# Attention's 64-partition products widened with zeros, and the compressed branch taken two heads at a time, in a hybrid decoder layer on one core

## The chip, the cores and the metric

The kernel runs on one core of one Trainium2 chip. TensorE (PE) multiplies matrices, with a queue of its own for weight loads; VectorE (DVE), ScalarE (ACT) and GpSimd (POOL) do elementwise work and reductions; SyncE (SP) issues most DMAs. The metric is device time in microseconds from one launch of the whole program, lower is better. Before, three runs took 3534.8, 3547.48 and 3551.98 us; the median is 3547.48 us.

## The reference

One decoder layer over 1024 tokens of width 1024, batch 1, in float32: a mixer of three branches, then a PEER feed-forward with 16384 experts. The change touches the first two branches of the mixer.

```python
h = rms_norm(x)
proj = h @ w_in
# A: stick-breaking attention, 8 heads of 64, strictly causal
z = einsum("bhtd,bhsd->bhts", q, k) * 64 ** -0.5
after = cumsum(log_1m, reverse) - log_1m         # log_1m = log_sigmoid(-z)
a = exp(log_sigmoid(z) + after);  o = a @ v
# B: sparse attention, 8 query heads of 64, 2 groups of keys and values
s_c = q @ kc * scale - slope * dist_c            # 63 compressed keys per group
p_c = softmax(where(valid_c, s_c, NEG));  o_c = p_c @ vc
imp = einsum("bgptc,cn->bgtn", p_c, overlap)     # 16 blocks of 64 keys, the best 4 taken
o_s = softmax(q @ k[selected] - slope * dist) @ v[selected]
o_w = softmax(q @ k[window of 256] - slope * dist) @ v[window]
o = g0 * o_c + g1 * o_s + g2 * o_w
# C: HGRN2 gated recurrence;  m = sum of gated branches @ W;  x = x + m @ w_out
x = x + peer(rms_norm(x));  out = rms_norm(x)
```

## The kernel before

Tokens are cut into four parts of 256, and a part into two tiles of 128. The program has a **mixer**, in which all three branches, their projections, the output projection and the routing of the feed-forward are interleaved, and a **dense part** behind it, which multiplies 512 tokens (parts 1 and 2) with all experts. The other 512 tokens gather their experts' rows from memory one by one (L1145 and L1155 issue the gathers on POOL, L1147 and L1157 use the rows on VectorE), spread over the mixer and the dense part.

Projections (`proj`, L258) multiply 128 x 128 weight blocks with 256 tokens as three float16 products each. Attention is in float32. In a float32 product TensorE gets one instruction of the program, which the profile shows as two pairs of weight load and product; a transpose is one pair.

Order comes from three places. `sb_items`, `nsa_items` and `hg_items` give lists of items of up to four stages (logits, weights, turned, values). At step t the planner's loop runs stage 0 of item t, stage 1 of item t-1, stage 3 of item t-3 and stage 2 of item t-2, in that order. Between steps it fills in projections and routing as *pieces*, by a running account of how much TensorE and VectorE have been given. The gathers' uses on VectorE are tied to steps. Last, the framework's scheduler decides the order on each engine, and it derives the waits between engines from what each instruction reads and writes.

What the change touches:

- **Stick-breaking heads.** A pair of heads p is projected at once: `pq` (L375) copies the 128 x 256 result to `q`, head 0 on partitions 0 to 63 and head 1 on 64 to 127. `k` has the same form. `logits` (L410) multiplies the 64 partitions of one head with up to 512 keys into `z`; where the chunk holds the diagonal a bfloat16 mask product (L412) adds to it.
- **Sparse heads, queries and keys.** For a group of four heads `qh` has 81 partitions: 0 to 63 hold the query (L550), 64 to 80 hold 17 rows that give each token a penalty per block and are multiplied only with `ksel`, whose rows 64 to 80 name the block. `kwin` and `kcT` (window and compressed keys) have 64 partitions, so L659 and L571 read `qh[0:64]`; L663 reads `qh[0:81]`.
- **A tile's items** (`res` in `nsa_items`): item 0 does the compressed branch, with `c_logits` (L571), `c_norm`, `c_turn` (L617, one transpose per head, 64 compressed keys to the partitions, copied by ACT in L619) and `c_values` (L624, one product of 64 x 64 per head); item 1 selects blocks; item 2 is the first window head; item 3 holds `c_rows` alone, as stage 2: it transposes the selection (L611) and adds it to a `base` of the part into rows 64 to 80 of `qh` (L612, VectorE). Window heads (L659) 1 to 3 and the four selected heads (L663) are items 4 to 10.
- **`turn_values`** copies the compressed values of both groups to `vc` (L527) and loads `base` for the part (L528).

In the names, `ns3g1t0` is part 3, group 1, tile 0; `b2h1` is the window branch and head 1, `b1` the selected branch; `tre` and `eT` are a head's transposed weights, `ob` its output, `trp` and `pT` the transposed compressed weights, `ovc` the compressed output, `trs` the transposed selection.

## Time and profile before

| what | us |
|---|---|
| runs, lowest, median and highest | 3534.8, 3547.48, 3551.98 |
| the profiled execution | 3542.42 |
| its span, first to last instruction | 3540.6 |
| PE busy (20660 instructions) | 3248.8, 92% |
| PE weight loads busy | 2179.3, 62% |
| DVE busy (6662) | 3001.0, 85% |
| ACT busy (3162) | 1549.5, 44% |
| POOL busy (1166) | 1357.0, 38% |
| chain of waits that ended last: PE, DVE, issue, DMA | 52%, 23%, 8%, 8% |

Busy times are of the profiled execution. Products overlap in TensorE's pipeline, and a row's duration runs from the start of the product to its modelled end; what a product holds back is read from the start of the next. A row of the timeline has start, duration, engine, line, operation, the names of output and inputs, the shape (for a product rows * columns of the weights, then the moving operand) and, after x, how many alike follow one another. The chain of waits goes back from the last instruction, at each step to what released it; its shares by line say which work stood on that path. "Issue" in it is time in which the engine waited for nothing that the profile shows.

### The profile page before, as it was taken

The page shows a single profiled execution, that of the slowest core. Times are in us where ns is not written, and L with a number is a line of the kernel's source. Part 1 is how long each engine was busy: PE and PEld are TensorE (multiplying, and loading weights), DVE is VectorE, ACT ScalarE, POOL GpSimd, SP SyncE. Part 2 cuts the span into 40 slices and gives each one's busy share as a digit, 9 for nine tenths or more (in the row PEclk, how much of TensorE's full clock was granted, in tenths as well). Part 3 has the DMA queues.
Part 4 walks back from the last instruction along what each step waited for, and adds up shares of the span by engine and source line. Part 5 has one row for each costly group of instructions (what it writes and reads, how often), then busy time and mean ns, then how long its engine had stood idle before and what let it go on. Part 6 is the DMA issues. An engine that isn't in the chain of part 4 may idle for free.

```text
span 3540.6 us, 57087 instructions
## 1 busy us (share of the span) xinstructions
PE 3248.8 (92%) x20660; PEld 2179.3 (62%) x20660; DVE 3001.0 (85%) x6662; ACT 1549.5 (44%) x3162; POOL 1357.0 (38%) x1166
## 2 busy tenths in 40 slices
PE   7999999999997799999879889879999999999997
PEld 6887777777876687887666654434444444444443
DVE  6665679888789888889998878999987998898898
ACT  5776455654443454644355333233333333233332
POOL 0000001343333233223332234347764765776663
PEclk9999999999997799999677899989999999999998
DMA  8964856889977587887665899779998999999997
GB/s 305 335 239 145 304 185 226 325 306 325 354 268 240 175 299 264 313 327 275 213 204 202 301 361 333 241 265 387 387 369 315 371 381 353 378 348 361 347 369 258
DMA packets 359336, 1058.07 MB, mean 299 GB/s; under 512 B 35238, under 2 KB 107626, under 8 KB 354444
## 3 DMA queue, kind: packets, MB, share of 16 engines
q0 software_dynamic: 147456, 536.94, 42.3%
q1 hardware_dynamic: 206988, 483.93, 38.6%
q10 hardware_dynamic: 4608, 33.56, 2.4%
q8 instruction: 162, 2.65, 0.3%
q14 instruction: 122, 1.00, 0.1%
HBM read 944.19 MB, written 110.10 MB: 298 GB/s over the span
## 4 chain that ended last, share of the span: by engine, by line
PE 52%; DVE 23%; issue 8%; DMA 8%; ACT 6%; POOL 2%; SPq 0%; DVEq 0%; ACTq 0%; POOLq 0%
PE g L258 13%; PE acc L1436 10%; PE pj_mg L258 4%; DVE gacc L1157 4%; PE g L1436 3%; DVE u L1147 3%; DMA v<-in_peer_v_dram,gidx 3%; PE pj_r_hg L258 2%; DMA u<-in_peer_u_dram,gidx 2%; PE pb L258 2%; PE pj_wo L258 2%; DMA gt<-d_G 1%; POOL u L1145 1%; PE z_sb L410 1%; DVE sv L980 1%
## 5 line engine op out<-in xcount | busy, mean ns | idle before, releaser
L1155 POOL DMA_INDIRECT v<-in_peer_v_dram,gidx x421 | 551.9, 1311 | 685.6 <-DVE gacc L1157 400.8
L1145 POOL DMA_INDIRECT u<-in_peer_u_dram,gidx x417 | 520.7, 1249 | 646.2 <-DVE u L1147 415.8
L258 PE MATMUL g<-h,us 128*128 128x512 f16 x3072 | 693.0, 383 | 22.8 <-DVE ts L982 7.9
L1157 DVE SCALAR_TENSOR_TENSOR gacc<-v,act,gacc 128x1024 f32<-128x1024 f32 x421 | 537.9, 1278 | 37.4 <-DMA v<-in_peer_v_dram,gidx 32.9
L1436 PE MATMUL acc<-vs,ac 128*128 128x512 f16 x2304 | 536.9, 381 | 20.4 <-ACT vs L213 8.4
L1436 PEld LDWEIGHTS <-ac 128*128 128x128 f16 x3072 | 302.0, 98 | 410.8 <-issue 50.3
L258 PEld LDWEIGHTS <-us 128*128 128x128 f16 x3072 | 302.5, 99 | 392.4 <-issue 22.2
L1147 DVE SCALAR_TENSOR_TENSOR u<-u,gh 128x1024 f32<-128x1024 f32 x417 | 501.8, 1217 | 27.3 <-DMA u<-in_peer_u_dram,gidx 26.0
L1395 ACT ACTIVATE ge<-g 128x512 f32<-128x512 f32 x128 | 76.1, 595 | 528.6 <-PE g L258 461.6
L258 PE MATMUL pj_mg<-hT,w_mg 128*128 128x256 f16 x2304 | 274.0, 274 | 4.8 <-ACT mg L881 3.7
L258 PEld LDWEIGHTS <-w_mg 128*128 128x128 f16 x2304 | 227.1, 100 | 35.9 <-issue 9.9
L1436 PE MATMUL g<-vs,ac 128*128 128x512 f16 x768 | 184.4, 383 | 22.7 <-ACT ge L1395 21.8
L214 DVE SCALAR_TENSOR_TENSOR vs<-vraw,vs 128x1024 f16<-128x1024 f32 x128 | 154.9, 1216 | 25.6 <-ACT vs L213 25.4
L213 ACT ACTIVATE vs<-vraw 128x1024 f16<-128x1024 f32 x128 | 132.6, 1046 | 88.6 <-DMA vraw<-in_peer_v_dram 88.5
L1145 POOL DMA_INDIRECT rr_u<-in_peer_u_dram,gidx x95 | 137.3, 1445 | 84.2 <-DVE rr_u L1147 61.0
L213 ACT ACTIVATE ac<-ge 128x512 f16<-128x512 f32 x128 | 80.1, 628 | 201.6 <-DVE ge L1429 155.6
L1155 POOL DMA_INDIRECT rr_v<-in_peer_v_dram,gidx x90 | 131.3, 1459 | 93.9 <-DVE gacc L1157 69.6
L214 DVE SCALAR_TENSOR_TENSOR us<-uraw,us 128x1024 f16<-128x1024 f32 x128 | 155.5, 1216 | 6.3 <-ACT us L213 5.0
L258 PE MATMUL pb<-o,w_b 128*128 128x256 f16 x1152 | 144.5, 282 | 16.2 <-DVE sg L919 10.5
L1219 PE MATMUL gb<-hot 128*128 128x128 f16 x512 | 126.0, 294 | 32.2 <-DVE hot L1216 26.2
L1429 DVE TENSOR_TENSOR ge<-ge,gt 128x256 f32<-128x256 f32 x256 | 98.0, 419 | 57.2 <-ACT ge L1395 27.2
L258 PE MATMUL pj_r_hg<-hT,w_r_hg 128*128 128x256 f16 x1152 | 140.2, 279 | 5.2 <-ACT iv_hg L739 3.3
(1141 smaller groups left out, 6361.5 us busy)
## 6 DMA issues: line engine op xcount, KB each, us to landing
uraw<-in_peer_uT_dram SPq DMA_DIRECT2D x128, 512.0 KB
vraw<-in_peer_v_dram SPq DMA_DIRECT2D x128, 512.0 KB
w_mg<-dw SPq DMA_DIRECT2D x72, 512.0 KB
gt<-d_G SPq DMA_DIRECT2D x32, 1024.0 KB
d_G<-stages ACTq DMA_DIRECT2D x20, 1024.0 KB
w_r_hg<-dw SPq DMA_DIRECT2D x36, 512.0 KB
w_b<-dw SPq DMA_DIRECT2D x72, 256.0 KB
wr_mg<-in_wblk_dram SPq DMA_DIRECT2D x24, 512.0 KB
```

The source lines that it names most:

```text
L213: S.activation(hi, src, AF.Copy, scale=scale)
L214: V.scalar_tensor_tensor(lo, in0=src, scalar=scale, in1=hi, op0=ALU.mult, op1=ALU.subtract)
L258: P.matmul(ps, l[:, k, :], r[:, k, :], start=(i == 0), stop=(i == n - 1))
L410: P.matmul(x["z"], st["q"][b:b + 64, tl * 128:(tl + 1) * 128], st["k"][b:b + 64, r0 + c0:r0 + c1], start=True, stop=(c0 > 0))
L1145: G.indirect_dma_start(out=ur, out_offset=None, in_=a["peer_u"], in_offset=bass.IndirectOffsetOnAxis(ap=idx[:, c:c + 1], axis=0))
L1147: V.scalar_tensor_tensor(ur, in0=ur, scalar=1.0, in1=h2, op0=ALU.mult, op1=ALU.mult, accum_out=hpre[:, c:c + 1])
L1155: G.indirect_dma_start(out=vr, out_offset=None, in_=a["peer_v"], in_offset=bass.IndirectOffsetOnAxis(ap=idx[:, c:c + 1], axis=0))
L1157: V.scalar_tensor_tensor(acc, in0=vr, scalar=act[:, c:c + 1], in1=acc, op0=ALU.mult, op1=ALU.add)
L1219: P.matmul(ps[:, n, :], hs[:, 0, :, n], hs[:, 2, :, n], start=True, stop=False)
L1395: S.activation(ge, ps, AF.Gelu, scale=1.0 / (SW * SH2))
L1429: V.tensor_tensor(gv, gv, gt[:, :, i % 8, :], op=ALU.mult)
L1436: P.matmul(ps, ac[:, x, t * 128:(t + 1) * 128], v[:, y, dh * 512:(dh + 1) * 512], start=start and n == 0, stop=stop and n == 2)
```

## The change

Four tiles are made once and cleared: `kwin` and `kcT` grow to 81 partitions with zeros in the new ones; `qh` is one tile for the whole program; `qz` holds the queries of a pair of stick-breaking heads in two planes, head 0 in partitions 0 to 63 of plane 0 and head 1 in 64 to 127 of plane 1, zeros elsewhere; `vc` holds the compressed values twice, on partitions 0 to 63 for the first of two heads and on 64 to 127 for the second, with zeros in the other blocks. Then

- L410 multiplies 128 partitions (`qz` with both heads' keys), and `pq` makes two copies of 64 partitions instead of one of 128;
- L571 and L659 multiply all 81 partitions of `qh`;
- `c_turn` transposes two heads (128 columns) at once, twice, and `c_values` multiplies two heads with the two blocks of `vc`, twice;
- `base` is loaded once, for positions within a tile, with a column of the tile's offset; `c_rows` adds three terms instead of two, and moves from stage 2 to stage 3 of its item, since the window logits of its tile now read the rows that it writes.

```diff
+        load(base, a["c_base"])
...
-    kwin = per.tile([64, 2, 512], F32, name="kwin")
+    kwin = per.tile([81, 2, 512], F32, name="kwin")
+    qh = per.tile([81, 4, PARTS[0].n], F32, name="qh")
+    qz = per.tile([128, 2, PARTS[0].n], F32, name="qz")
+    vc = per.tile([128, 2, 128], F32, name="vc")
+    base = per.tile([17, 136], F32, name="base")
+    for t in (kwin[64:81], qh[64:81], qz, vc):
+        G.memset(t, 0.0)
...
-    kcT = per.tile([64, 2, 64], F32, name="kcT")
+    kcT = per.tile([81, 2, 64], F32, name="kcT")
...
-            st["q"] = W2(f"q_{nm}", (128, pt.n), tag="sbq", bufs=1)
-            S.activation(st["q"], ps, AF.Copy, scale=0.125 * PS)
+            for hh in range(2):
+                S.activation(qz[hh * 64:hh * 64 + 64, hh], ps[hh * 64:hh * 64 + 64], AF.Copy, scale=0.125 * PS)
...
-                P.matmul(x["z"], st["q"][b:b + 64, tl * 128:(tl + 1) * 128], st["k"][b:b + 64, r0 + c0:r0 + c1], start=True, stop=(c0 > 0))
+                P.matmul(x["z"], qz[:, hh, tl * 128:(tl + 1) * 128], st["k"][:, r0 + c0:r0 + c1], start=True, stop=(c0 > 0))
...
-            V.tensor_copy(st["vc"], pv)
-            st["base"] = load(per.tile([17, n], F32, tag="base", name=f"base_{nm}"), a["c_base"][:, t0:t0 + n])
+            V.tensor_copy(vc[0:64, :, 0:64], pv)
+            V.tensor_copy(vc[64:128, :, 64:128], pv)
...
-                P.matmul(zc[:, i, :], st["qh"][0:64, i, ts], kcT[:, g, :], start=True, stop=True)
+                P.matmul(zc[:, i, :], qh[:, i, ts], kcT[:, g, :], start=True, stop=True)
...
-            V.tensor_tensor(st["qh"][64:81, :, ts], kv["base"][:, ts].unsqueeze(1).to_broadcast([17, 4, 128]), tr[0:17, :].unsqueeze(1).to_broadcast([17, 4, 128]), op=ALU.add)
+            V.scalar_tensor_tensor(qh[64:81, :, ts], in0=base[:, 0:128].unsqueeze(1).to_broadcast([17, 4, 128]), scalar=base[:, 128 + ti:129 + ti], in1=tr[0:17, :].unsqueeze(1).to_broadcast([17, 4, 128]), op0=ALU.add, op1=ALU.add)
...
-            for i in range(4):
-                P.transpose(trp[:, i, :], x["s"][:, i, :], ident)
+            for i in range(2):
+                P.transpose(trp[:, i, :], x["s1"][:, 1 + i * 128:129 + i * 128], ident)
...
-            for i in range(4):
-                P.matmul(ovc[:, i, :], x["pT"][:, i, :], kv["vc"][:, g, :], start=True, stop=True)
+            for i in range(2):
+                P.matmul(ovc[:, 2 * i:2 * i + 2, :], x["pT"][:, i, :], vc[:, g, :].rearrange("p (h d) -> p h d", h=2), start=True, stop=True)
...
-        res = [[c_logits, c_norm, c_turn, c_values], [None, c_select, None, None], None, [None, None, c_rows, None]]
+        res = [[c_logits, c_norm, c_turn, c_values], [None, c_select, None, None], None, [None, None, None, c_rows]]
...
-                                P.matmul(zv[:, a:b], st["qh"][0:64, i, ts], kwin[:, g, k0:k0 + b - a], start=True, stop=True)
+                                P.matmul(zv[:, a:b], qh[:, i, ts], kwin[:, g, k0:k0 + b - a], start=True, stop=True)
```

The scheduler's order on TensorE, at tile 0 of group 1 in part 3, from the transposed compressed weights to the first selected logits. Before (the shape is the output's):

```order
L617 MATMUL trp_ns3g1t0_20107<-packed_106,s_ns3g1t0_19957 64x128 x4
L659 MATMUL z_ns3g1t0b2h2_0_20209<-kwin_152,qh_ns3g1_19470 128x384
L624 MATMUL ovc_ns3g1t0_20143<-vc_ns3_15966,pT_ns3g1t0_20112 128x64 x4
L683 MATMUL tre_ns3g1t0b2h0_0_20191<-packed_106,e_ns3g1t0b2h0_0_20089 128x128 x3
L611 MATMUL trs_ns3g1t0_20218<-packed_106,sel_ns3g1t0_20098 32x128
L659 MATMUL z_ns3g1t0b2h3_0_20222<-kwin_152,qh_ns3g1_19470 128x384
```

and now:

```order
L621 MATMUL trp_ns3g1t0_20109<-packed_106,s_ns3g1t0_19950 128x128 x2
L663 MATMUL z_ns3g1t0b2h2_0_20142<-kwin_152,qh_153 128x384
L663 MATMUL z_ns3g1t0b2h3_0_20152<-kwin_152,qh_153 128x384
L687 MATMUL tre_ns3g1t0b2h0_0_20124<-packed_106,e_ns3g1t0b2h0_0_20091 128x128 x3
L628 MATMUL ovc_ns3g1t0_20115<-vc_155,pT_ns3g1t0_20112 128x128 x2
L615 MATMUL trs_ns3g1t0_20157<-packed_106,sel_ns3g1t0_20100 32x128
```

Four transposes and four products have become two of each, and the logits of the last window head stand ahead of the transposed selection instead of behind it. (Line numbers of the changed kernel are four higher here.)

On VectorE, at the first tile of the program, around the write of the selection rows (`og` is the gated output of the compressed branch, `w_r2` and `o2` are splits of a weight and of another branch's output, `e` and `nmx` the reduction of a window head). Before:

```order
L626 TENSOR_TENSOR og_ns0g0_897<-ovc_ns0g0t0_1071,gts_ns0_442 128x256
L214 SCALAR_TENSOR_TENSOR w_r2_hg1_0_1219<-wr_r2_hg1_0_1220,w_r2_hg1_0_1219 128x1024
L214 SCALAR_TENSOR_TENSOR o2_0_1022<-sq_hg0_0_967,o2_0_1022 128x256
L612 TENSOR_TENSOR qh_ns0g0_817<-base_ns0_815,trs_ns0g0t0_1173 17x4x128
L668 ISA e_ns0g0t0b2h3_0_1212,nmx_ns0g0t0b2h3_1209<-z_ns0g0t0b2h3_0_1210,dwin_140 128x128
```

and now:

```order
L630 TENSOR_TENSOR og_ns0g0_903<-ovc_ns0g0t0_1075,gts_ns0_450 128x256
L221 SCALAR_TENSOR_TENSOR w_r2_hg1_0_1208<-wr_r2_hg1_0_1209,w_r2_hg1_0_1208 128x1024
L221 SCALAR_TENSOR_TENSOR o2_0_1028<-sq_hg0_0_973,o2_0_1028 128x256
L672 ISA e_ns0g0t0b2h3_0_1244,nmx_ns0g0t0b2h3_1241<-z_ns0g0t0b2h3_0_1242,dwin_140 128x128
L616 SCALAR_TENSOR_TENSOR qh_153<-base_156,trs_ns0g0t0_1247 17x4x128
```

The row write has moved behind the reduction of the last window head. Over the whole program VectorE's gather rows stand at the same places as before: between the row writes of any two tiles their count so far differs by at most four, and 417 of 1024 stand ahead of the first of the dense part's rows in both.

More of the change, by code (lines that the diff above doesn't have):

```diff
@@ L519, in compress @@
                 P.matmul(pk[:, :, 0:ncb], st["cw", which][:, j, :], st["xp", which][:, j, :, 0:ncb], start=(j == 0), stop=(j == 15))
-            V.tensor_copy(dst[:, :, c0:c1], pk[:, :, 0:ncb])
+            V.tensor_copy(dst[0:64, :, c0:c1], pk[:, :, 0:ncb])
         def turn_values():
-            st["vc"] = SM(f"vc_{nm}", [64, 2, 64], bufs=1)
             pv = ps_mm.tile([64, 2, 64], F32, tag="mm", name=f"pvc_{nm}")
@@ L544, in pq @@
         def pq(i):
-            if i == 0:
-                st["qh"] = W2(f"qh_{gn}", (81, 4, pt.n), tag="qh", bufs=1)
             ps = proj(B_NQ + 2 * g + i, hTs[pt.i], f"nq{i}_{gn}", pt)
             for u in range(2):
-                S.activation(st["qh"][0:64, 2 * i + u, :], ps[u * 64:u * 64 + 64, :], AF.Copy, scale=0.125 * PS / SLOPES[4 * g + 2 * i + u])
+                S.activation(qh[0:64, 2 * i + u, :], ps[u * 64:u * 64 + 64, :], AF.Copy, scale=0.125 * PS / SLOPES[4 * g + 2 * i + u])
         return [lambda: pq(0), lambda: pq(1)]
@@ L611, in c_rows @@
             P.transpose(tr[0:32, :], x["sel"], ident)
-            V.tensor_tensor(st["qh"][64:81, :, ts], kv["base"][:, ts].unsqueeze(1).to_broadcast([17, 4, 128]), tr[0:17, :].unsqueeze(1).to_broadcast([17, 4, 128]), op=ALU.add)
+            V.scalar_tensor_tensor(qh[64:81, :, ts], in0=base[:, 0:128].unsqueeze(1).to_broadcast([17, 4, 128]), scalar=base[:, 128 + ti:129 + ti], in1=tr[0:17, :].unsqueeze(1).to_broadcast([17, 4, 128]), op0=ALU.add, op1=ALU.add)
         def c_turn():
-            trp = ps_tr.tile([64, 4, 128], F32, tag="tr", name=f"trp_{tn}")
-            for i in range(4):
-                P.transpose(trp[:, i, :], x["s"][:, i, :], ident)
-            x["pT"] = W2(f"pT_{tn}", (64, 4, 128))
+            trp = ps_tr.tile([128, 2, 128], F32, tag="tr", name=f"trp_{tn}")
+            for i in range(2):
+                P.transpose(trp[:, i, :], x["s1"][:, 1 + i * 128:129 + i * 128], ident)
+            x["pT"] = W2(f"pT_{tn}", (128, 2, 128))
             S.activation(x["pT"], trp, AF.Copy)
@@ L662, in logits @@
                         last = c1 == W
-                        P.matmul(zv, st["qh"][0:81, i, ts], ksel[0:81, g, c0:c1], start=True, stop=not last)
+                        P.matmul(zv, qh[:, i, ts], ksel[0:81, g, c0:c1], start=True, stop=not last)
                         if last:
@@ L1489, in _constants @@
     tt = np.arange(T)
-    b = np.zeros((17, T), f)
-    b[0:16] = 64 * np.arange(16)[:, None] - tt[None, :]
-    b[16] = 1
+    b = np.zeros((17, 136), f)
+    b[0:16, 0:128] = 64 * np.arange(16)[:, None] - np.arange(128)[None]
+    b[0:16, 128:136] = -128 * np.arange(8)[None]
+    b[16, 0:128] = 1
     c["c_base"] = b
```

## The prediction

> **What bounds the kernel now.** I read first the span and the busy time by stretch, then the chain of waits in the stretches where the changed lines run, and last the timeline of TensorE around single changed products. The profiled execution took 3542.42 us, its span is
>
> ```profile
> span 3540.6 us, 57087 instructions
> ```
>
> and the busy times by stretch are (each engine's busy us and instructions: PE, its weight loads, DVE, ACT, POOL; then granted clock, DMA share, GB/s):
>
> ```profile
> 0.00:500.00 500.00, 451.48 (x3786) 385.27 (x3787) 303.23 (x747) 316.35 (x733) 5.81 (x68) 0.97 0.73 256
> 500.00:1200.00 700.00, 633.49 (x4814) 522.12 (x4813) 620.64 (x1984) 332.70 (x833) 223.68 (x242) 0.92 0.79 275
> 1200.00:1600.00 400.00, 384.28 (x3031) 322.09 (x3031) 332.21 (x676) 211.10 (x503) 125.16 (x120) 0.97 0.83 295
> 2400.00:3541.00 1141.00, 1103.52 (x5077) 498.09 (x5074) 1037.44 (x1397) 374.59 (x505) 721.01 (x505) 0.99 0.96 355
> ```
>
> All lines that change run in the mixer, before 2000 us; the dense part behind it keeps its instructions. In the mixer two engines compete. Up to 500 us TensorE is busy 90% and VectorE 61%: TensorE leads. From 500 to 1200 us both stand near 90%, and who is late changes from piece to piece. From 1200 to 1600 us TensorE leads again with 96% against 83%. So an instruction taken off TensorE is worth its time in the first and third stretch, and little where VectorE's top-k and gather rows are late. The chain of waits, its shares by line in the whole mixer, then in the first and in the third stretch, says how much:
>
> ```profile
> by line: issue 9.5%; PE pj_mg L258 7.1%; PE pj_r_hg L258 4.1%; DVE u L1147 3.8%; DMA u<-in_peer_u_dram,gidx 3.5%; PE pb L258 3.1%; PE pj_wo L258 2.6%; DVE gacc L1157 2.5%; POOL u L1145 1.9%; PE z_sb L410 1.8%; PE pj_q_sb L258 1.4%; PE gb L1
> by line: PE pj_mg L258 13.0%; PE pj_r_hg L258 9.3%; PE pj_wo L258 4.2%; PE pb L258 3.8%; issue 3.1%; PE pj_i_hg L258 2.7%; PE pj_q_sb L258 2.7%; PE z_sb L410 2.2%; PE pj_k_sb L258 2.1%; PE pj_nq_ns0g L258 2.1%; PE pj_v_sb L258 2.1%; ACT L89
> by line: PE pj_mg L258 11.7%; PE pb L258 7.3%; PE gb L1219 5.5%; PE gb L1220 5.3%; PE pj_r_hg L258 3.3%; DVE gacc L1157 3.1%; PE z_sb L410 3.0%; PE ov_sb L440 2.7%; PE pj_wo L258 2.6%; DMA v<-in_peer_v_dram,gidx 2.6%; PE pj_q_sb L258 2.4%;
> ```
>
> The largest changed line, L410 (the logits of the stick-breaking heads), is busy in the stretches as follows (TensorE, weight loads, clock, DMA):
>
> ```profile
> 0.00:500.00 500.00, 13.59 (x40) 5.89 (x40) 0.97 0.73 256
> 500.00:1200.00 700.00, 33.01 (x64) 10.55 (x64) 0.92 0.79 275
> 1200.00:1600.00 400.00, 21.69 (x44) 6.68 (x44) 0.97 0.83 295
> 1600.00:2000.00 400.00, 28.86 (x44) 7.70 (x44) 0.78 0.67 226
> ```
>
> Of its 97.1 us, 1.8% of 2000 us = 36 us lie on the chain. In the first stretch it is 2.2% of 500 = 11 of 13.6 us (0.81), in the third 3.0% of 400 = 12 of 21.7 us (0.55), and in the other two together 13 of 61.9 us (0.21).
>
> **What a product on 64 partitions costs.** Two places of the timeline, TensorE alone (start, duration, line, shapes; "64*128" is rows times columns of weights; a float32 product takes two instructions). Durations overlap in the pipeline, so I use differences of starts:
>
> ```profile
> 1438.05 0.94 PE L683 MATMUL tre_ns3g0t0b1h<-packed,e_ns3g0t0b1h 128*128 128x128 f32 x7
> 1438.92 1.12 PE L410 MATMUL z_sb<-k_sb,q_sb 64*128 64x512 f32 x2
> 1439.97 0.23 PE L412 MATMUL z_sb<-sbmask,identb 128*128 128x128 bf16 x1
> ...
> 1592.51 0.62 PE L683 MATMUL tre_ns3g0t1b1h<-packed,e_ns3g0t1b1h 128*128 128x128 f32 x4
> 1592.97 1.02 PE L663 MATMUL z_ns3g0t1b1h<-ksel,qh_ns3g 81*128 81x512 f32 x2
> 1593.83 0.22 PE L665 MATMUL z_ns3g0t1b1h<-cmask,identb 128*128 128x128 bf16 x1
> ```
>
> Both pairs stream the same 512 columns. On 64 rows it takes 1439.97 - 1438.92 = 1.05 us, on 81 rows, which already use the whole array, 0.86 us. Weights of 64 rows are loaded only when the array stands still; those of 81 rows come in under the product before. The work ahead pays too: a transpose of 128 columns takes 0.108 us (four in 0.43 us, L617 below), so seven should take 0.76 and take 0.87 (0.11 more), four should take 0.43 and take 0.46 (0.03 more). A run of 64-row products therefore costs (1.05 + 0.11) - (0.86 + 0.03) = **0.27 us** more than the same columns on the whole array.
>
> The compressed branch, one tile:
>
> ```profile
> 1405.31 0.60 PE L617 MATMUL trp_ns3g0t<-packed,s_ns3g0t 128*64 128x128 f32 x4
> 1405.74 1.47 PE L258 MATMUL pb<-o,w_b 128*128 128x256 f16 x12
> 1407.14 0.91 PE L659 MATMUL z_ns3g0t0b2h<-kwin,qh_ns3g 64*128 64x384 f32 x2
> ...
> 1410.73 1.47 PE L258 MATMUL pb<-o,w_b 128*128 128x256 f16 x12
> 1412.14 1.10 PE L624 MATMUL ovc_ns3g0t<-vc_ns,pT_ns3g0t 64*128 64x64 f32 x8
> 1413.17 0.87 PE L683 MATMUL tre_ns3g0t0b2h<-packed,e_ns3g0t0b2h 128*128 128x128 f32 x6
> 1413.88 1.47 PE L258 MATMUL pb<-o,w_b 128*128 128x256 f16 x12
> 1415.19 1.67 PE L663 MATMUL z_ns3g0t0b1h<-ksel,qh_ns3g 81*128 81x512 f32 x4
> ...
> 1531.78 0.60 PE L258 MATMUL pj_v_sb<-hT,w_v_sb 128*128 128x256 f16 x4
> 1532.31 1.10 PE L571 MATMUL zc_ns3g0t<-kcT,qh_ns3g 64*128 64x64 f32 x8
> 1533.34 0.49 PE L849 MATMUL ov_hg<-att_hg,iv_hg 128*128 128x128 f32 x2
> ```
>
> Twelve projections ahead of an 81-row product take 1.31 us, ahead of a 64-row one 1.40 and 1.41: the same stop of 0.1 us.
>
> **The change, part by part.**
>
> 1. Stick-breaking logits (L410): 192 instructions are 96 products, nearly all alone between other work: 96 x 0.27 = 25.9 us of TensorE.
>
> 2. Window logits (L659): between these two rows, the first and the last, I count 54 unbroken runs with whole-array work on both sides: 54 x 0.27 = 14.6 us.
>
> ```profile
> 85.78 0.48 PE L659 MATMUL z_ns0g0t0b2h<-kwin,qh_ns0g 64*128 64x128 f32 x2
> 1888.04 1.65 PE L659 MATMUL z_ns3g1t1b2h<-kwin,qh_ns3g 64*128 64x384 f32 x2 [0.44 <-DVE nmx_ns3g1t1b2h L668]
> ```
>
> 3. Compressed logits (L571), 16 tiles: eight instructions take 1.03 us where eight loads of 128 columns need 0.86, and the four projections ahead take 0.53 instead of 0.44: 0.26 x 16 = 4.2 us.
>
> 4. Compressed values (L624), 16 tiles: the stop of 0.10 and 1.03 us go; two products of 128 columns, four instructions of 0.108 us, come: 0.70 x 16 = 11.2 us.
>
> 5. Transposed weights (L617): two transposes instead of four, 2 x 0.108 x 16 = 3.5 us.
>
> The sum is **59 us** of TensorE, all in the mixer. That the added rows are zeros or hold finite numbers against zero keys changes no duration: the product streams columns, as the 81-row pair shows.
>
> Added work. The query copy of L375 becomes two copies of 64 partitions, at the price (min/median/max ns) of the nearest row, L550, which copies the same shape:
>
> ```profile
> L550 ACT ACTIVATE qh_ns0g<-pj_nq_ns0g x8: 378/379/382, 75.2 to 204.6; 64x256 f32<-64x256 f32 x8
> ```
>
> There are 16 of these copies, so that is 16 x 0.38 = 6 us more on ACT, which is busy 63% of the first stretch and about half of the next two; the copy is made ahead of its logits by the planner. I cost it at nothing, with 6 us as the other end. The copy of the transposed weights halves in width, and three small loads of `base` fall away, so neither takes it up again. Four more small copies and four clears at the start are too few to count.
>
> The wait. Compressed and window logits now read rows 64 to 80 of the queries too, so the write of the selection rows (L612) has to follow the window logits of its tile; it is moved one stage back for that. In before it often starts while the last of these runs:
>
> ```profile
> 1567.89 0.91 PE L659 MATMUL z_ns3g0t1b2h<-kwin,qh_ns3g 64*128 64x384 f32 x2
> 1568.61 0.68 DVE L612 TENSOR_TENSOR qh_ns3g<-base_ns,trs_ns3g0t 17x512 f32<-17x512 f32 x1
> 1570.98 1.04 PE L663 MATMUL z_ns3g0t1b1h<-ksel,qh_ns3g 81*128 81x512 f32 x2
> ```
>
> The logits end at 1568.80, so the row write would start 0.2 us later and end at 1569.49, still 1.5 us ahead of the selected logits (L663) that wait for it. Behind it on VectorE stands a gather row, and behind that the window logits' own reduction. Bounds: nothing, if every tile has this cover; 16 x 0.91 = 15 us of VectorE, if each waited for a whole product. The row above is nearest to nothing; I take 1 us. The operation also changes from a sum of two to a sum of three at the same 17 x 512; no row shows that shape, and I take it as equal, with a doubling (16 x 0.68 = 11 us of VectorE, in the stretches where VectorE leads perhaps half of it) as the other end. On VectorE the gathers keep their places among the row writes to within four, so pacing does not shift.
>
> **How much of the 59 us arrives.** L410 is busy longer late in the mixer, where its rows are long; but what it saves goes by the run, not by the length. By runs (20 in the first stretch, 22 in the third, 54 in the others) its share on the chain is (20 x 0.81 + 22 x 0.55 + 54 x 0.21) / 96 = **0.41**. I take this for the other lines too, which come once or a few times a tile: 0.41 x 59 = 24 us, less 1 for the wait: **23 us**. From the profiled execution that gives 3519; the three runs shown have a median 5 us above it, 3547.5, so the forecast for a median is **3524**. If 15 to 40 us arrive, it lies between 3507 and 3532.
>
> **The rivals.**
>
> *VectorE takes the slack.* From 500 to 1200 us it is busy 621 of 700 us and TensorE 633; TensorE's lead there is hardly 13 us, about what L410 alone loses in that stretch (32 x 0.27 = 9 us). If the same happens in the first stretch through ACT and DMA, only the third keeps its part, 0.55 of 13 us (22 x 0.27 = 6 of L410, and a fifth of the other lines' 33), and with VectorE's possible 6 us for row writes nothing is left: 0 to 10 us, 3537 to 3553. Against it: in the first stretch VectorE is 39% idle. Chance 0.22.
>
> *Nearly all of it arrives.* If what I call off the chain only waits in turn with it, 45 to 59 us go: 3488 to 3503. For it: TensorE is above 90% nearly everywhere. Chance 0.10.
>
> *The change does only part of what it says:* the second weight load of a product still waits for the first product. Then a third of each 0.27 us stays, 150 runs x 0.09 = 13.5 us, and 0.41 of 45 us less 1 arrives, 17 us: 3530. The row of 81 rows speaks against it, since 0.86 us leaves no room for a load between its two halves. Chance 0.03. The Trainium skill states a rule of this kind (TensorE: Matmul & The Clock Gate, Part 3, "The mechanism"): weight loads overlap products in flight only when they go to another row group. By that rule whole-array loads would never overlap, and padding would not help inside a pair; the twelve projections in 1.31 us say otherwise for whole-array weights.
>
> *Slower, by the clock.* In these two rows (columns as above) VectorE leads, and in the second TensorE has fallen to a granted clock of 0.59:
>
> ```profile
> 1000.00:1100.00 100.00, 93.65 (x763) 78.03 (x761) 96.48 (x396) 42.83 (x108) 30.75 (x27) 1.00 0.79 275
> 1100.00:1200.00 100.00, 70.61 (x311) 53.16 (x311) 93.80 (x291) 42.00 (x106) 27.39 (x32) 0.59 0.50 157
> ```
>
> Less work on TensorE means more gaps there. If the first of them fell to 0.59 as well, its 93.7 us of TensorE would need 159, up to 65 us more; less the 23 that is 42 us slower: 3589. It decides from about two thirds of such a stretch on (23 + 18 of 65 us). Against it: what is taken off in 100 us of that kind is about 3 us, and where VectorE leads the clock is not paid in full. Chance 0.08.
>
> **How the numbers follow.** The forecast has 0.57, then 0.10, 0.22, 0.03 and 0.08 for the rivals in the order nearly all, VectorE, part, slower. A measurement of this kernel tells 0.5% (18 us) from no change. Faster by more than that is most of the forecast (0.50), nearly all (0.10) and some of "part": 0.62. Within it are the rest of the forecast, VectorE's case and the rest: 0.30. Slower: 0.08. The range leaves out the slower case and half of "nearly all": 3495 to 3553.
>
> **What would show it.** In the profile of the changed kernel a pair of 512 columns in L410's place should take 0.86 us from start to start, not 1.05, and the projections ahead of it should lose their 0.1 us. TensorE's work up to 2000 us should shrink by about 59 us at equal clock, and the dense part should begin some 23 us earlier and last as long. Wrong would be: selected logits that wait for the row write longer than the 1 us taken; a granted clock well below 0.97 before 500 us; or a mixer that is as long as before with more idle time on TensorE.

## The result, and the profile after

The changed kernel takes **3520.55 us** in the median of 8 runs (3510.71 to 3532.81), the kernel before 3549.73 in the median of 8 runs beside them: a ratio of **0.9924, 95% interval 0.99 to 0.9949**, that is 27 us or 0.76% less. The profiled execution of the changed kernel took 3510.71 us, the lowest of its runs, so what follows from it alone is off by some microseconds. (In one run below, "stops put in elsewhere", one of six executions took 15322 us, and its ratio goes by the other five, 3504 to 3531 us.)

Its span and the busy times by stretch (columns as before: PE, weight loads, DVE, ACT, POOL, then granted clock, DMA share, GB/s):

```profile
span 3508.9 us, 56926 instructions
...
0.00:500.00 500.00, 445.14 (x3778) 388.44 (x3779) 306.70 (x768) 319.56 (x740) 8.51 (x72) 0.96 0.73 258
500.00:1200.00 700.00, 617.71 (x4836) 523.92 (x4835) 623.10 (x1975) 343.93 (x856) 226.06 (x243) 0.92 0.80 278
1200.00:1600.00 400.00, 381.23 (x3134) 330.73 (x3133) 346.19 (x708) 223.59 (x529) 137.73 (x131) 0.99 0.88 308
1600.00:2000.00 400.00, 321.72 (x2110) 257.93 (x2109) 358.10 (x1035) 170.84 (x376) 120.61 (x103) 0.81 0.66 229
```

TensorE's busy time fell in every stretch (451 to 445, 633 to 618, 384 to 381 us), while the instructions of all engines moved ahead: between 1200 and 1600 us TensorE now does 3134 instead of 3031. Busy time per window can't show more than that, because a faster program has other work in the same window. So I compare when the same work starts in the two profiles. The projection that started at 473 us starts 3.4 us earlier, the one at 1089 us 10 us, the one at 1375 us 27 us, the one at 1694 us 29 us, and the first product of the dense part (2062 us) 26 us. Most of the gain over the kernel before thus comes between 500 and 1375 us, and little before 500 us.

The chain of waits by line, of the mixer and of its first 500 us:

```profile
by line: issue 8.5%; PE pj_mg L265 7.2%; DVE u L1151 4.5%; PE pj_r_hg L265 3.7%; DMA u<-in_peer_u_dram,gidx 3.5%; DVE gacc L1161 2.7%; PE pb L265 2.1%; POOL u L1149 2.1%; PE pj_wo L265 2.0%; DMA v<-in_peer_v_dram,gidx 1.9%; PE gb L1223 1.7%
by line: PE pj_mg L265 12.1%; PE pj_r_hg L265 7.2%; PE pj_wo L265 4.2%; PE pj_q_sb L265 3.0%; issue 3.0%; PE pj_xc_ns L265 2.6%; DMA ksel<-in_c_kblk_dram 2.5%; ACT L902 2.3%; DMA dw<-w_ng_ns 2.1%; PE pj_nq_ns0g L265 2.1%; DMA sg<-d_g 2.0%; 
```

`z_sb` (L410, now L417) is gone from the first lines of both, where it had 1.8% and 2.2%; DVE's gather rows L1151 rose from 3.8 to 4.5% of the mixer, and three DMAs stand in the first stretch's list.

The same products as before on TensorE (start, duration, line, shapes), each read from the start of the next:

```profile
1384.60 0.81 PE L663 MATMUL z_ns3g0t0b2h<-kwin,qh 81*128 81x384 f32 x2
1385.25 0.38 PE L621 MATMUL trp_ns3g0t<-packed,s_ns3g0t 128*128 128x128 f32 x2
1385.47 0.49 PE L687 MATMUL tre_ns3g0t0b2h<-packed,e_ns3g0t0b2h 128*128 128x128 f32 x3
1385.80 2.78 PE L265 MATMUL pb<-o,w_b 128*128 128x256 f16 x24
1388.42 0.81 PE L663 MATMUL z_ns3g0t0b2h<-kwin,qh 81*128 81x384 f32 x2
1389.07 0.61 PE L628 MATMUL ovc_ns3g0t<-vc,pT_ns3g0t 128*128 128x128 f32 x4
1389.51 1.47 PE L265 MATMUL pb<-o,w_b 128*128 128x256 f16 x12
...
1417.14 0.50 PE L687 MATMUL tre_ns3g0t0b1h<-packed,e_ns3g0t0b1h 128*128 128x128 f32 x3
1417.47 1.02 PE L417 MATMUL z_sb<-k_sb,qz 128*128 128x512 f32 x2
1418.33 0.22 PE L419 MATMUL z_sb<-sbmask,identb 128*128 128x128 bf16 x1
```

The 512-column pair takes 1418.33 - 1417.47 = 0.86 us and the transposes ahead of it 0.33 for three, 0.11 each: the stop of 0.27 us is gone. 24 projections ahead of window logits take 2.62 us, 0.109 each, with no stop either. Two transposes take 0.22 us, the compressed values 0.44 instead of 1.03 us and a stop. The edits do on TensorE what the prediction said.

Where, then, is the rest? The longest waits of TensorE in the mixer, first of the changed kernel, then of the kernel before (line waiting, what it waits for: us in total, times, longest):

```profile
PE z_sb L417 <- DVE r_sb L432: 32.2, 14, 13.4
PE tra_sb L438 <- ACT r_sb L433: 19.3, 14, 3.7
...
PE pb L265 <- DVE sg L923: 14.4, 11, 2.2
```

```profile
PE z_sb L410 <- DVE r_sb L425: 31.2, 12, 11.7
...
PE tra_sb L431 <- ACT r_sb L426: 9.7, 8, 2.9
...
PE pb L258 <- DVE sg L919: 8.1, 6, 2.8
```

TensorE waits twice as long for ACT's part of the stick-breaking heads, and nearly twice as long for VectorE's gates `sg`. To see the whole of it I divided TensorE's time up to the last output projection of the mixer (about 2100 us), from the start of each product to the start of the next: the time that its columns need at full clock; gaps in which the engine waited; what it took longer while the granted clock was half; and the rest, mostly stops. (Worked out from all rows of TensorE, each kernel's from one execution. The wait until the first product is left out; it is 7 us longer in the changed kernel and in the two below.)

| us | columns | stops, rest | half clock | waits |
|---|---|---|---|---|
| before | 1647.5 | 119.1 | 150.9 | 196.0 |
| changed | 1636.7 | 85.2 | 127.5 | 230.4 |
| infra (below): changed, but all products as before | 1647.5 | 119.3 | 143.1 | 210.3 |
| no padding (below) | 1636.7 | 119.5 | 141.6 | 205.0 |

45 us of columns and stops went, 23 us of half clock too, and 34 us came back as waits, 7 more at the start: 27 us in all. Of the 34, 24 are waits for ACT (80 before, 105 now), 6 for VectorE (113, 119) and 5 for DMAs.

### The profile page after: what moved, and what is told of

Same layout as the page of the kernel before. It is cut to its first block, busy times and chain, and to the rows that moved or that the text cites. A ratio compares the mean times of both kernels' runs of the same rounds, so it can differ in the third digit from the quotient of the medians.

```text
span 3508.9 us, 56926 instructions
## 1 busy us (share of the span) xinstructions
PE 3176.1 (91%) x20564; PEld 2166.0 (62%) x20564; DVE 2999.3 (85%) x6666; ACT 1554.1 (44%) x3179; POOL 1357.4 (39%) x1170
## 4 chain that ended last, share of the span: by engine, by line
PE 47%; DVE 28%; DMA 10%; issue 7%; ACT 6%; POOL 2%; SPq 0%; ACTq 0%; DVEq 0%; POOLq 0%
PE g L265 13%; PE acc L1440 9%; DVE u L1151 4%; PE pj_mg L265 4%; DVE gacc L1161 3%; PE g L1440 3%; DMA v<-in_peer_v_dram,gidx 2%; PE pj_r_hg L265 2%; DMA u<-in_peer_u_dram,gidx 2%; PE pj_wo L265 1%; DMA vraw<-in_peer_v_dram 1%; DMA gt<-d_G 1%; PE pb L265 1%; POOL u L1149 1%; DVE rr_u L1151 1%
## 5 line engine op out<-in xcount | busy, mean ns | idle before, releaser
L1151 DVE SCALAR_TENSOR_TENSOR u<-u,gh 128x1024 f32<-128x1024 f32 x417 | 504.0, 1223 | 42.0 <-DMA u<-in_peer_u_dram,gidx 41.6
L265 PEld LDWEIGHTS <-w_b 128*128 128x128 f16 x1152 | 116.5, 102 | 42.9 <-issue 21.1
```

The lines of the kernel that those rows point to most:

```text
L265: P.matmul(ps, l[:, k, :], r[:, k, :], start=(i == 0), stop=(i == n - 1))
L1151: V.scalar_tensor_tensor(ur, in0=ur, scalar=1.0, in1=h2, op0=ALU.mult, op1=ALU.mult, accum_out=hpre[:, c:c + 1])
```

## The experiments

Ratios are to the kernel before, with the 95% interval; 0.001 is 3.5 us.

An edit of the products changes one thing more: the scheduler derives its waits from what is read and written, and orders the engines anew. I compared the order of instructions in the traces, up to 2200 us. Between the changed kernel and "no padding" some 1150 of 14870 instructions stand elsewhere on TensorE, and 470 of 4760 operations on VectorE; between the two runs with the write in the third stage it is 1420 and 670. "Parts 1 to 3 alone" (120 and 30), "stops, with the wait" (130 and 60) and "65 rows" (40 and 40) have nearly the order of the changed kernel. Where the order moves, a difference of some microseconds can come from that as well, and no run here holds it fixed.

**No padding.** The changed kernel with the logits of L417, L575 and L663 on 64 partitions; everything else stays.

```diff
-P.matmul(x["z"], qz[:, hh, ...], st["k"][:, ...], ...)
+P.matmul(x["z"], qz[b:b + 64, hh, ...], st["k"][b:b + 64, ...], ...)
-P.matmul(zc[:, i, :], qh[:, i, ts], kcT[:, g, :], ...)
+P.matmul(zc[:, i, :], qh[0:64, i, ts], kcT[0:64, g, :], ...)
-P.matmul(zv[:, a:b], qh[:, i, ts], kwin[:, g, k0:k0 + b - a], ...)
+P.matmul(zv[:, a:b], qh[0:64, i, ts], kwin[0:64, g, k0:k0 + b - a], ...)
```

> The changed kernel with its padding undone in the products alone: stick-breaking, compressed and window logits multiply 64 partitions again (of the same tiles), and everything else of the change stays (two heads at a time in the compressed branch, one query tile, two query copies, the moved row write). Theory (the time came from the stops of TensorE at 64-row products): the stops of the stick-breaking and window logits (96 and 54 runs of 0.27 us) and of the compressed logits (16 of 0.26) are back, 45 us of TensorE, of which 0.41 to 0.5 counts: 18 to 22 us slower than the changed kernel, a ratio to before of 0.997 to 0.998. Rival (the rest of the change brought the time): as fast as the changed kernel, 0.992. Rival (a lucky order of the scheduler): anything, with the stops in the timeline and no loss.

Measured 0.9965 (0.9948 to 0.9983), 3540.46 us. The timeline of TensorE shows the stop again, 1.05 us for the pair:

```profile
1439.31 1.12 PE L417 MATMUL z_sb<-k_sb,qz 64*128 64x512 f32 x2
1440.36 0.23 PE L419 MATMUL z_sb<-sbmask,identb 128*128 128x128 bf16 x1
```

So the padding is worth 0.9965 - 0.9924 = 0.0041, 15 us (the intervals of both together allow 4 to 25), for 44.7 us of TensorE, less than the theory had. The third expectation, a lucky order, is not ruled out for the size, since the order moved too.

**Stick-breaking alone.** The kernel before with `qz` and L410 on 128 partitions, and nothing else of the change.

```diff
+qz = per.tile([128, 2, PARTS[0].n], F32, name="qz")   # cleared
-P.matmul(x["z"], st["q"][b:b + 64, ...], st["k"][b:b + 64, ...], ...)
+P.matmul(x["z"], qz[:, hh, ...], st["k"][:, ...], ...)
```

> The kernel before with the padded stick-breaking queries alone (two query copies, whole-array product). Theory: 96 stops of 0.27 us are gone, 26 us of TensorE, so 11 to 13 us faster than before, ratio 0.9963 to 0.9970. Rival (the compressed branch and the moved row write brought the time): 1.000.

Measured 0.9973 (0.9955 to 0.9991): 10 us (3 to 16) of 25.9 arrive, 0.37, near the share of 0.41.

**Pairs alone.** The kernel before with the compressed weights turned and multiplied two heads at a time.

```diff
+vc = per.tile([128, 2, 128], F32, name="vc")   # cleared, values on both halves
-for i in range(4):  P.transpose(trp[:, i, :], x["s"][:, i, :], ident)
+for i in range(2):  P.transpose(trp[:, i, :], x["s1"][:, 1 + i * 128:129 + i * 128], ident)
-for i in range(4):  P.matmul(ovc[:, i, :], x["pT"][:, i, :], kv["vc"][:, g, :], ...)
+for i in range(2):  P.matmul(ovc[:, 2 * i:2 * i + 2, :], x["pT"][:, i, :], vc[:, g, :]..., ...)
```

> The kernel before with two heads at a time in the compressed branch alone (two transposes and two products of 128 columns in place of four and four; this takes the values' product off 64 rows as well). Theory: 15 us of TensorE less, so 6 to 7 us faster than before, ratio 0.998. Rival (this part brought the time): 20 us faster or more, 0.994 or below.

Measured 0.996 (0.9942 to 0.9978): 14 us (8 to 21), about all of the 14.7 us of TensorE that it takes out, more than expected.

**Stops put in elsewhere.** The changed kernel with the selected logits on 64 rows, which leaves out the rows that select and that give the distance.

```diff
-P.matmul(zv, qh[:, i, ts], ksel[0:81, g, c0:c1], ...)
+P.matmul(zv, qh[0:64, i, ts], ksel[0:64, g, c0:c1], ...)
```

> A dose in the other direction: the changed kernel with the selected logits on 64 partitions, which leaves the selection and distance rows out of that branch. No instruction is more or less, but each of about 75 runs of selected logits now stops TensorE. Theory: 75 x 0.27 = 20 us more on TensorE, of which 0.41 to 0.5 counts: 8 to 10 us slower than the changed kernel, ratio to before about 0.995, and the pair of 512 columns takes 1.05 us from start to start in place of 0.86. Rival (the stops don't matter, since TensorE waits elsewhere then): as the changed kernel, 0.992.

Measured 0.9907 (0.9874 to 0.9939): no loss, although the stops are there. But without the rows these products need not wait for the row write either, so this run mixes two things. The run "stops, with the wait" below takes them apart.

**Write in the third stage.** The changed kernel with `c_rows` back in stage 2.

```diff
-[None, None, None, c_rows]
+[None, None, c_rows, None]
```

> The changed kernel with one thing put back: the write of the selection rows (c_rows, L612) stands in the third of the four stages again, as before the change, so that the selected logits have a stage between the write and their use. Theory of the prediction: the later place costs 1 us at most (bounds 0 to 15), so the ratio to the kernel before stays at 0.9921 to 0.9926 (changed kernel 0.9924), and the selected logits' wait for the write is short in both. Rival: the wait is the reason why only part of the 59 us arrives; then 0.988 to 0.990 here. Second rival: the later place is itself a gain (the write stands less in VectorE's way); then 0.994 or more.

Measured 0.9978 (0.996 to 0.9997): 19 us (8 to 30) slower than the changed kernel, which neither the theory nor the first rival had; it lies in the second rival's range. For the row write L616 the profile lists who waited for it (us, times), and the list of TensorE's waits adds a line on its transpose:

```profile
who waited for it (us, times):
  PEld z_ns2g0t0b2h L663: 1.1, 1
  PEld z_ns2g1t0b2h L663: 1.1, 1
  PE z_ns2g0t0b2h L663: 0.9, 1
  PE z_ns2g1t0b2h L663: 0.9, 1
...
```

```profile
PE trs_ns2g1t L615 <- DVE sel_ns2g1t L610: 3.1, 2, 2.7
```

The window logits (L663) wait for the rows, which they read only because of the padding. These waits of TensorE are some 5 us. Its time at half clock is 434 us against 403 in the changed kernel, which is up to 15 us of work; how the one may follow from the other is told below. The last run here tests whether the dependence or the place is the cause.

**Padding in part 0 alone, and in parts 1 to 3 alone.** The changed kernel with all three kinds of logits on 81 or 128 rows in part 0 only, and in the other run everywhere but in part 0.

```diff
+PADDED = lambda i: i == 0          # the other run: i > 0
+qp = slice(0, 128) if PADDED(pt.i) else slice(b, b + 64)    # L417; 81 or 64 rows in L575 and L663
```

> The changed kernel with the whole-array logits products in part 0 alone (the first 500 us or so; some 42 of the 166 runs of 64-row products, 11 us of TensorE time), and 64 rows in the other three parts. With 64 rows in all parts the ratio was 0.9965, with none 0.9924. By the shares of the prediction (0.81 before 500 us) part 0 brings 9 us: 0.9940. By the profile of the changed kernel, whose lead is 3 us at 470 us, it brings at most 3 us: 0.9957 to 0.9965.

> The changed kernel with the whole-array logits products in parts 1 to 3 alone (from about 500 us on; some 124 of the 166 runs, 33 us of TensorE time), and 64 rows in part 0. By the shares of the prediction the 33 us bring about 0.4 of themselves less part 0's 9 us, so about 10 us over the 0.9965 of the kernel with 64 rows in all parts: 0.994 to 0.995. By the profile of the changed kernel nearly all of the padding's 14.6 us lies here: 0.9924 to 0.993.

Measured 0.9994 (0.998 to 1.0008) for part 0 alone, and 0.9927 (0.9913 to 0.9941) for parts 1 to 3. With none it was 0.9965, with all 0.9924. So the padding of parts 1 to 3 brings 13 us (5 to 22), about all that padding brings, and that of part 0 on top of it 1 us, with 10 either way. Alone the padding of part 0 even loses 10 us (2 to 18) against none, though it takes 11 us of stops away. By these medians the effects don't add up: the two alone make 3 us, and all padding 15. That gap of 11 us has an interval of 13 either way, so it is likely and not shown.

**Stops, with the wait.** The changed kernel with the selected logits on 64 rows, but for the first product of each tile, which keeps its 81 rows and the wait.

```diff
+qp = slice(0, 81 if i == 0 and c0 == 0 else 64)
-P.matmul(zv, qh[:, i, ts], ksel[0:81, g, c0:c1], ...)
+P.matmul(zv, qh[qp, i, ts], ksel[qp, g, c0:c1], ...)
```

> The changed kernel with the selected logits on 64 rows, except the first product of the first head of each tile, which keeps its 81 rows and so the wait for the selection rows. The selection and distance rows are left out for the other heads. Some 70 runs of 64-row products come in, at 0.27 us each 19 us of TensorE time. Theory: a stop costs what a removed one brought, 0.3 to 0.4 of 19 us, so 6 to 8 us over the changed kernel: 0.9942 to 0.9948. Rival 1: the selected logits stand where TensorE waits for VectorE or a free logits buffer anyway, so the stops cost nothing there: 0.9915 to 0.993. In the run that left all the rows out, the time was 0.9907 with the wait for the rows gone; if that wait was what paid for the stops, this kernel, which has it, is slower than that by 5 us or more (0.992 and above).

Measured 0.9955 (0.9939 to 0.997), 11 us slower than the changed kernel (1 to 21) for some 19 us of stops, and 17 us (4 to 30) slower than the run without the wait. Two products of one tile on TensorE:

```profile
1408.96 2.78 PE L265 MATMUL pb<-o,w_b 128*128 128x256 f16 x24
1411.68 1.12 PE L668 MATMUL z_ns3g0t0b1h<-ksel,qh 64*128 64x512 f32 x2
1412.73 0.43 PE L699 MATMUL ob_ns3g0t0b2h<-vwin,eT_ns3g0t0b2h 128*128 128x64 f32 x2
```

The pair takes 1.05 us and the 24 projections ahead 2.72 instead of 2.62: the same stop in a place where it was not before, and time is lost, somewhat more than the 6 to 8 us expected. The stop has its price there too; rival 1 falls. This is the cleanest of the tests by dose, since the order is nearly that of the changed kernel. That the run without the wait lost nothing fits the second rival, but no wait of TensorE for the rows shows in the changed kernel (below), and that run has another order (1340 instructions elsewhere), so by which way it gained stays open.

**65 rows.** The changed kernel with L575 and L663 on 65 rows.

```diff
-P.matmul(zv[:, a:b], qh[:, i, ts], kwin[:, g, k0:k0 + b - a], ...)
+P.matmul(zv[:, a:b], qh[0:65, i, ts], kwin[0:65, g, k0:k0 + b - a], ...)
```

> The changed kernel with the compressed and the window logits on 65 rows instead of 81: 64 of the head and one of zeros. Theory: the stop goes with the use of more than 64 rows, that is of both halves of the array, so the runs of these products have no excess over the sum of their columns' times (5 ns or less in the median, as with 81 rows), and the time is the changed kernel's, 0.99 to 0.995. Rival: the stop shrinks with the rows or needs the full array; then 0.2 to 0.29 us a run stay, in about 70 runs.

One execution: 3526.57 us. One row of zeros is enough. Over the window logits' runs the excess above the columns' time is 5 ns in the median, where 64 rows have 290; one of them, 384 columns in 0.70 us:

```profile
1375.59 0.81 PE L663 MATMUL z_ns3g0t0b2h<-kwin,qh 65*128 65x384 f32 x2
1376.29 1.48 PE L265 MATMUL pb<-o,w_b 128*128 128x256 f16 x12
```

**Four values on 128 rows.** The kernel "pairs alone", with the values still one head at a time, on 128 rows of the zero-padded tile: no stop, but four products of 64 columns.

```diff
-for i in range(2):  P.matmul(ovc[:, 2 * i:2 * i + 2, :], x["pT"][:, i, :], vc[:, g, :]..., ...)
+for i in range(4):  P.matmul(ovc[:, i, :], x["pT"][:, i // 2, :], vc[:, g, 64 * (i % 2):64 * (i % 2) + 64], ...)
```

> The kernel before with the compressed weights turned two heads at a time, and the values still one head at a time, but on 128 rows: four products of 64 columns against the zero-padded values, instead of two of 128. Of the some 15 us of TensorE time that the whole edit takes out (its ratio was 0.996), four products of 64 columns in place of two of 128 keep 16 x 0.44 = 7 us. Theory TensorE time: half of the 14 us is lost, 0.998. Rival: what arrived is the stop of the 64-row products and the shorter way from the weights to the gated values, and the seven microseconds lay beside other work: 0.9955 to 0.9965.

Measured 1.0009 (0.9992 to 1.0027): neither expectation. The timeline shows the products as costed, two of 64 columns in 0.49 and 0.40 us, where two of 128 columns take 0.44:

```profile
1421.17 0.66 PE L626 MATMUL ovc_ns3g0t<-vc,pT_ns3g0t 128*128 128x64 f32 x4
1421.66 1.47 PE L260 MATMUL pb<-o,w_b 128*128 128x256 f16 x12
1422.97 0.56 PE L626 MATMUL ovc_ns3g0t<-vc,pT_ns3g0t 128*128 128x64 f32 x4
1423.37 0.27 PE L613 MATMUL trs_ns3g0t<-packed,sel_ns3g0t 128*32 128x128 f32 x1
```

7 us more on TensorE than "pairs alone" cost 17 us (8 to 26), and the stops and transposes that it does save brought nothing. As between the parts, a microsecond of TensorE has no fixed price.

**All products as before (infra).** The changed kernel with 64-row logits and with the compressed branch one head at a time: the resident query tiles, the second query copy, the sum of three terms, the single load of offsets and the later row write stay.

```diff
 # "no padding", and
-for i in range(2):  P.transpose(trp[:, i, :], x["s1"][:, 1 + i * 128:129 + i * 128], ident)
+for i in range(4):  P.transpose(trp[:, i, :], x["s"][:, i, :], ident)
-for i in range(2):  P.matmul(ovc[:, 2 * i:2 * i + 2, :], x["pT"][:, i, :], vc[:, g, :]..., ...)
+for i in range(4):  P.matmul(ovc[:, i, :], x["pT"][:, i, :], vc[0:64, g, 0:64], ...)
```

> The changed kernel with both kinds of products put back: all logits on 64 rows, compressed weights and values one head at a time. What stays of the change is what it needs beside them: resident query tiles, two copies of the queries for one, the three-term sum, the offsets loaded once, and the write of the selection rows after the window logits. Theory of the prediction: this costs nothing to 1 us, so 0.9995 to 1.0005; then the kernel with 64-row logits (0.9965) and the one with the pairs alone (0.996) differ by nothing. Rival: the later write is a gain by itself, as the 0.9978 of the kernel with the write put back seems to say (0.9924 without): 0.994 to 0.996.

Measured **1.0034 (1.0016 to 1.0052)**: what the change needs beside its products costs 12 us (6 to 18). Both expectations fall, the rival's most clearly. Against this kernel, the pairs bring 24 us (0.9965; 16 to 33) and pairs and padding together 39 us (0.9924; 28 to 50).

**Write in the third stage, window logits on 64 rows.**

```diff
-[None, None, None, c_rows]
+[None, None, c_rows, None]
-P.matmul(zv[:, a:b], qh[:, i, ts], kwin[:, g, k0:k0 + b - a], ...)
+P.matmul(zv[:, a:b], qh[0:64, i, ts], kwin[0:64, g, k0:k0 + b - a], ...)
```

> The changed kernel with the write of the selection rows in the third stage again, and the window logits on 64 rows, so that they don't read the rows that are written. With the write in the third stage and the window logits on 81 rows the ratio was 0.9978. Theory: that loss is the window logits' wait for the rows, which they read only because of the padding; here it is gone, and the stops of the window logits come back (14.6 us of TensorE time at 0.4, so 4 to 6 us): 0.9935 to 0.995. Rival: the loss comes from the place of the write itself, whose transpose holds TensorE up for the selection: 0.997 to 1.000.

Measured 0.9931 (0.9905 to 0.9958), 17 us faster than with the padded window logits in this order (5 to 28). In the program the row write is where it was in that run; only the window logits no longer read its rows. For L616 the profile now lists

```profile
who waited for it (us, times):
  PEld z_ns2g0t0b1h L667: 0.4, 1
  PE z_ns2g0t0b1h L667: 0.2, 1
```

So the loss goes with the dependence and not with the write's place in the list of items. The way is not shown: the waits that were seen made up some 5 us of it, and without the dependence the scheduler orders the engines anew. And since this kernel is as fast as the changed one, padding the window logits and moving the write for it gains nothing that these runs can tell from doing neither.

## Why a microsecond of TensorE has no fixed price

The half clock multiplies small waits. The record of the granted clock has steps of 3.41 us, in which it is 1.00 or 0.50. Here is the same wait of 2.1 us, for the same weights (`aT_sb`), in the kernel before and in "infra"; first TensorE's row with its wait in the kernel before, then in "infra", there with the projections that follow:

```profile
131.62 0.43 PE L440 MATMUL ov_sb<-v_sb,aT_sb 128*128 128x64 f32 x2 [2.12 <-ACT aT_sb L433]
```

```profile
134.12 0.43 PE L447 MATMUL ov_sb<-v_sb,aT_sb 128*128 128x64 f32 x2 [2.11 <-ACT aT_sb L440]
...
134.87 4.23 PE L265 MATMUL pj_r_hg<-hT,w_r_hg 128*128 128x256 f16 x22
139.03 0.70 PE L417 MATMUL z_sb<-k_sb,qz 64*128 64x256 f32 x2
```

And the clock's steps around it, again before and then "infra" (window, its length, TensorE's busy us and instructions, granted clock, DMA share, GB/s):

```profile
127.70:131.10 3.40, 1.80 (x17) 1.00 0.97 375
131.10:134.50 3.40, 2.85 (x24) 1.00 0.62 211
```

```profile
131.70:135.10 3.40, 1.25 (x10) 1.00 0.67 269
135.10:138.50 3.40, 3.40 (x18) 0.50 0.97 296
```

Before, the wait lies across two steps, 1.60 us in one and 0.55 in the other, and the clock stays. In "infra" all of it falls into one step, and the next runs at half: 22 projections take 139.03 - 134.87 = 4.16 us where 22 of 0.109 need 2.40. The same wait costs 1.8 us more because it came 2.5 us later. Nothing in the kernel arranges how its waits fall against these steps.

Over five of the profiles (before, changed, no padding, parts 1 to 3, infra), from 60 to 2060 us, I counted the steps at full clock by the time in which TensorE streamed columns. Below 1.2 us, the next step was at half in all 104 cases. From 1.2 to 1.5 us in 15 of 57, from 1.5 to 1.8 in 12 of 95, from 1.8 to 2.1 in 2 of 143, above 2.1 in none of 2057. So what counts is how little is streamed within one step. Waits are one way to that, and not the only one. In "infra" the step at 189.7 us shows TensorE busy throughout, with 64-row products in it, and still the next is at half:

```profile
189.70:193.10 3.40, 3.40 (x18) 1.00 0.85 301
193.10:196.50 3.40, 3.40 (x18) 0.50 0.71 253
```

By the columns of its products some 2.0 us were streamed there.

The Trainium skill (TensorE: Matmul & The Clock Gate, Part 1 and "Why this matters for your kernels") has a window of 3413 ns and asks for no idle gaps above some 3 us between bursts, since one idle window brings the half clock back. The trace agrees on the window, 3.41 us, but not on the gap: here 2.11 us were enough, and in all the cases below 1.2 us of streaming in a step.

In the runs as a whole, the time at half clock goes roughly with the result. It was 403 us in the changed kernel, 396 to 412 in the five other kernels whose medians or single time lie at 3521 to 3533 us, and 422 to 439 in the kernel before and the seven others, which lie at 3535 to 3562 us. It doesn't order them within a group: "infra", the slowest of all, has 422 us, less than the kernel before with 428. That the clock causes the uneven prices is argued from these rows, and was not tested by itself: no run holds the clock fixed, nor the scheduler's order.

## Why the prediction was right, and where it was not

The time (3524 foretold, 3520.55 measured) and the sign were right, and the range held. The steps, one by one:

- **0.27 us a run of 64-row products: right.** In the changed kernel the pair takes 0.86 us and the work ahead has no stop; with 64 rows both come back at once (1.05 us), and in new places they come where rows are taken away (the selected logits).
- **59 us off TensorE: 45 us of it show.** These are columns and stops at full clock; how much of the rest went at half clock, the table doesn't tell.
- **The share on the chain, 0.41: mis-sized.** Against the kernel that has all of the change but its products, 39 us (28 to 50) of 59 arrive, 0.66. For the stick-breaking logits alone in the kernel before it was 0.37, for the pairs about 1 there and above 1 in the changed kernel (24 us for 14.7). The intervals are wide: 0.12 to 0.62 for the first, 0.5 to 1.4 for the second.
- **The added work, 1 us: mis-sized.** It costs 12 us (6 to 18). The bounds for its terms had reached 6 us for ACT's copies, 15 us for the wait and 11 us for the sum of three; I took 0, 1 and 0. The sum is not what cost: L616 takes 0.74 us instead of 0.68, 16 x 0.06 = 1 us. Neither is it the selected logits' wait for the write. In the changed kernel its row, VectorE's idle time before it, and who waited for it are

```profile
L616 DVE SCALAR_TENSOR_TENSOR qh<-base,trs_ns3g0t x2: 737/737/737, 1392.9 to 1533.4; 17x512 f32<-17x512 f32 x2
...
  PE trs_ns1g0t L615: 2.9, 1
  PE trs_ns2g0t L615: 1.3, 1
  PE trs_ns1g1t L615: 1.3, 1
...
  POOL u L1149: 1.2, 2
```

  so no product waits for it, and VectorE waits 5.5 us for the transposed selection. By the table, "infra" has 14 us more waits on TensorE than before, and all of it is for ACT (95 us against 80). The extra query copies, 6 us on ACT that I took as hidden, lie there, but the traces speak against them as the cause: for the copies themselves TensorE waits 2.5 us in "infra" and 0.7 before, and "pairs alone", which has no added copy, waits some 91 us for ACT as well. By 285 us "infra" is already 8 us late, with three steps at half clock since 60 us, where the kernel before has none; "pairs alone" has two of them. The four clears, which I left out as too few, are no answer either: all kernels that have them scale the first `x` on VectorE 7 to 8 us later (at 16.98 us in the changed kernel, 10.00 before) and start their first product as late, but the changed kernel and "infra" have made that up by the hundredth projection, at 36 us. So which of the added edits costs the 12 us stays open: they were not tried one by one.
- **So the net was right by two errors of opposite sign**: 24 - 1 = 23 foretold, 39 - 12 = 27 measured. That the time came so close is luck in part.
- **Where it arrives: wrong for the middle.** By the shares of L410 the first 500 us should have brought 0.81 of their stops, the stretch from 500 to 1200 us 0.21. The lead over the kernel before, 3 us at 473 us, holds the added work too: "infra" is 8 us behind the kernel before there, 11 at 1089 us and 7 at 1375 us. Against "infra" the changed kernel is 12 us ahead at 473 us, 21 at 1089 and 34 at 1375. The 12 us are about what 0.81 gives for the first stretch (11 us of padding and some 4 of the pairs), though the runs with and without the padding of part 0 show no such gain in the end. The 9 us up to 1089 are more than 0.21 gives (some 4 us), and so is what follows. The 17 us between 1089 and 1375 us, which the changed kernel gains on the kernel before, are not the padding's, for "no padding" gains 17 there too; in the changed kernel 14 of them are less time lost at half clock (41 us before, 27 now). What failed is the step from "this line is on the chain of waits" to "taking it off is worth that share". The chain names one path, and it doesn't hold what a change does to the order and the clock.
- **The wait: the reasoning was right, and its place mattered more than I said.** Window logits that read the rows must come ahead of the write. Done the other way, 19 us (8 to 30) are lost; the 15 us of my upper bound were for the order that I chose.
- **The rivals.** "VectorE takes the slack" named the wrong engine: 34 us did come back as waits, but 24 of them for ACT and 6 for VectorE, and less came back than went. "Nearly all of it arrives" holds for the pairs alone. "Slower, by the clock" had the right mechanism and the wrong sign here: the loss at half clock fell from 151 to 128 us, as fewer steps were at half. With part 0 alone the clock goes the other way: 439 us at half, against 427 with no padding at all. "The second weight load still waits" is out, by the 0.86 us. (The times given for "VectorE takes the slack", 3537 to 3553, also hold a loss of 6 us, which its "0 to 10 us" leaves out.)

## What to carry to other kernels

A float32 product on 64 rows among whole-array products costs a stop of some 0.29 us a run, and 65 rows, one of them zeros, are enough to lose it; but look at what the wider product reads, since it may now depend on a write that it didn't need, and that can cost more than the stop. A share on the chain of waits is no price: add or take the same cost in one stretch and see, and price the additions with a kernel that has them alone. Where an edit also moves the scheduler's order, and TensorE often streams for less than 2 us of a clock step, a change below half a per cent can come out at twice its price or at none: compare the order of two traces before you read such a difference as a price.

## What the hardware showed that I had not expected

- The half clock after a step with less than about 1.2 us of streaming, in all 104 cases, and its dependence on how a wait falls into the 3.41 us steps (above).
- 64-row products seem to count for less in it (as in the step at 189.7 us above). Among steps with 1.5 to 1.8 us of streaming, the clock fell in 8 of 11 that held 0.6 to 1.5 us of 64-row products, and in 3 of 78 that held none. These are few cases, and no run tested it.
- A float32 product of 64 columns takes as long as one of 128 (0.111 us an instruction against 0.109). Both load 128 columns of weights; the products of 32 columns on 64 columns of weights, L519, take 0.058, so the weight load seems to set it. That is why two heads at a time halve the values.
